# A hybrid decoder layer on one core: the scratch of rotated queries and keys laid out row by row, and TensorE and the SyncE queue issued in the order in which the program is written

## The chip, the core and the metric

The kernel runs on one core of a Trainium2 chip, in one launch. Its time is the device time in microseconds (us); several executions are timed, and one execution is recorded by the profiler. The engines are PE (TensorE; PEld is its loading of weights), DVE (VectorE), ACT (ScalarE), POOL (GpSimd) and SP (SyncE, which only issues transfers). ACT issues transfers too. Each engine works through its own list of instructions in order; 16 DMA engines carry out the transfers of all of them.

## The reference

One layer over 1024 positions of width 2048, in float32:

```python
h = rms_norm(x, norm_gain)
q, k, v, g_attn, xr, g_rec = jnp.split(h @ w_in, SPLITS, axis=-1)   # w_in: 2048 x 6144
q = rope(q.reshape(1, 1024, 8, 2, 64), cos, sin)                    # 8 heads, 2 maps of 64
k = rope(k.reshape(1, 1024, 8, 2, 64), cos, sin)
...                      # per head: w = softmax(q0 k0) - lam * softmax(q1 k1), causal
o = rms_norm(w @ v, subln_gain) * (1 - lam_init) * silu(g_attn)
r = rg_lru(causal_conv(xr, conv_w, conv_b), ...) * silu(g_rec)      # 8 blocks of 128
x = x + jnp.concatenate([o, r], -1) @ w_out                         # w_out: 2048 x 2048
return rms_norm(x, final_gain)
```

## The kernel before, in words

**Precision.** Every matmul operand is split into a rounded part (hi) and the rest (lo), and products are added as hi·hi, hi·lo and lo·hi, so a projection step of 128 inputs is three matmuls of 128x512 (`triple`, L364). `split` (L169) makes hi on ACT (L170) and lo on DVE or POOL (L171).

**Order of the work.** The sequence is handled in two halves of 512 positions (b = 0 and 1; the attention calls them l). In each half the units of `UNITS` come one after the other: a head (four projections: two for the rotated queries and keys, then values and gate) or a recurrent block (two projections). Afterwards `outputs` does the output projection (L829). A projection takes four tiles of weights of 256 KB; each tile serves 12 matmuls (four triples).

Around the projections stand small tasks that are Python generators: `Slots` counts ticks, one per triple, and every `yield n` puts the rest of a task n ticks later into the written order. The weight task `stream` (L256) issues loads up to 6 tiles ahead of the split (`WAHEAD`), and splits up to 4 tiles ahead of their use (`WRING`). All buffers of 128x512 come from one list of 89 slots.

**The path that the change touches.** `rope` (L460) takes the two projections of queries and keys of a head. Their 128 rows are four groups of 32: map 0 and map 1 of the queries, then map 0 and map 1 of the keys. It rotates them into two tiles and splits both: four tiles, hi of the first and second (t2, t4) and lo of the first and second (t1, t3). They go through a scratch in DRAM, `fs`, stored from ACT (L471), so that a map of a head comes back as one operand of 128 rows. Six ticks after the stores the head is ready; `loader` (L610) then calls `head_load` (L585), which issues on SP (all through `load`, L156) the two key tiles, one per map, and four query tiles: per map one of the hi rows and one of the lo rows, each with its 64 rows twice, read with a broadcast of 2. For l = 1 the keys and values of the first half are loaded again as well. `SCORE_LEAD` ticks later (24 or 28) `score` (L619) starts: per 128 positions, four or more matmuls into `sw` (L634 and L635; the second uses the lo queries), a masked maximum on DVE (L639), exponentials on ACT (L646), and on DVE the difference of the two softmaxes (L654). `weighted` (L679) then transposes the result in pairs of 128 positions (L758, into one bank, `tr`), splits it (L767, L768), and multiplies it with the values (L780 to L783). `head_out` (L718) normalises (L723, L726, L734, L737) and stores the rows `ms`.

**Who sets the order.** In the kernel before, a scheduler orders the instructions of each engine by its own model of time, with the written order as priority; so an engine's list can differ from the written one. The waits between engines and transfers are put in by the framework in either case.

Of the kernel before, what the change touches and what calls it, by code (L numbers as in the profile page):

```python
# [13 lines left out]
F32 = mybir.dt.float32  # L14
# [11 lines left out]
HALF = 512  # L26
# [81 lines left out]
class Trunk:  # L108
# [351 lines left out]
    def rope(self, b, h, ts):  # L460
        nc = self.nc
        t1, t2, t3, t4 = ts
        self.tt(t1.f, t1.f, t2.f, ALU.subtract)
        self.tt(t3.f, t3.f, t4.f, ALU.add)
        yield 1
        self.split(t1.f, t2, t1)
        self.split(t3.f, t4, t3)
        yield 4
        fs = self.dram.tile([4, 4, 32, HALF], F32, name=self.nm("fs"))
        for i, t in enumerate((t2, t4, t1, t3)):  # L470
            nc.scalar.dma_start(fs[:, i], t.f)  # L471
        self.rel(*ts)
        self.fs[h, b] = fs
        yield 6
        self.ready.add(("q", h, b))
# [109 lines left out]
    def head_load(self, h, l):  # L585
        k, q, v = [], [], []
        for c in range(l + 1):
            ks = []
            for m in range(2):
                kk = self.allocr()  # L590
                self.load(kk.f, self.fs[h, c][2 + m].rearrange("i r c -> (i r) c"))
                ks.append(kk)
            k.append(ks)
        for i in (0, 2):
            for m in range(2):
                t = self.allocr()
                src = self.fs[h, l][m, i:i + 2].rearrange("i r c -> (i r) c")
                self.load(t.f, src.unsqueeze(0).broadcast_to([2, 64, HALF]))
                q.append(t)
        if l:  # L600
            vs = []
            for d in self.vsc[h]:
                t = self.allocr()
                self.load(t.f, d)
                vs.append(t)
            v.append(vs)
        self.hd[h, l] = (k, q, v)
        self.loaded[h, l] = self.sl.now
# [261 lines left out]
            self.rel(y)  # L870

    def run(self):
        if True:
            self.consts()
            for gen in (self.stream(), self.loader(), self.scores(), self.weighted()):
                self.sl.spawn(gen)
            for b in range(2):
                for name in UNITS:
                    (self.head if name[0] == "h" else self.rec)(b, int(name[1]))
                self.final(b)  # L880
                self.outputs(b)
# [58 lines left out]
```

## Time and profile before

| | |
|---|---|
| time, median of 3 runs | 2099.34 us (2096.14 to 2101.21) |
| time of the profiled execution | 2100.45 us |
| its span, from the first to the last instruction | 2098.7 us |
| mean granted TensorE clock | 0.913 of full speed |
| busy: PE, PEld, DVE, ACT, POOL | 82%, 67%, 37%, 38%, 40% |
| moved by the DMA engines | 237.02 MB, 113 GB/s in the mean |
| loads from the scratch `fs` (SP) | 112 of 256 KB |
| stores to it (ACT) | 64 of 256 KB |

How to read it: PE is the busiest engine, but an average over stages; its idle time stands in stretches whose ends the profile puts down to a releaser, an engine or a transfer. The granted clock is that of TensorE alone, at one of two levels, 1.2 or 2.4 GHz (0.5 or 1.0 of full speed), so that a mean of 0.913 says that it was at the lower level for some 17% of the time.

### The profile page before, as it was taken

How to read it: one execution, taken by the hardware profiler on the slowest of the kernel's cores; microseconds unless marked ns; L12 is line 12 of the kernel's file. 1: busy time of each engine (PE TensorE's matmuls, PEld its weight loads, DVE VectorE, ACT ScalarE, POOL GpSimd, SP SyncE). 2: the span in 40 equal slices, each digit the busy share in tenths (PEclk: the TensorE clock that was granted, in tenths of full speed). 3: DMA queues.
4: the chain of work that ended last, by engine and by line, in shares of the span. 5: the costliest groups of instructions: out<-in, count | busy, mean ns of one | idle time of the engine just before them, and what ended most of it. 6: DMA issues, size and time to landing. Idle time of an engine off the chain costs nothing.

```text
span 2098.7 us, 22044 instructions
## 1 busy us (share of the span) xinstructions
PE 1724.3 (82%) x7716; PEld 1408.4 (67%) x7716; DVE 779.1 (37%) x1333; ACT 804.7 (38%) x1393; POOL 849.8 (40%) x710
## 2 busy tenths in 40 slices
PE   7758868787786779989979787878787879799996
PEld 5646756566665667768867576767676767587885
DVE  8515342414151325741115242424252515265101
ACT  6215242525161236633414342525252424365321
POOL 7313433434342325765632242424233333266560
PEclk9879989898898889999989898989898999899998
DMA  5432333333323235423652242323233232255312
GB/s 209 135 112 74 109 97 110 94 105 93 120 79 120 79 98 170 159 81 99 214 185 84 79 119 81 113 90 113 91 106 97 90 115 83 89 181 188 113 63 80
DMA packets 131502, 237.02 MB, mean 113 GB/s; under 512 B 13248, under 2 KB 17472, under 8 KB 131392
## 3 DMA queue, kind: packets, MB, share of 16 engines
q1 hardware_dynamic: 116032, 206.27, 31.6%
q10 hardware_dynamic: 15360, 29.36, 4.0%
q8 instruction: 60, 0.98, 0.2%
q14 instruction: 50, 0.41, 0.1%
HBM read 197.83 MB, written 37.75 MB: 112 GB/s over the span
## 4 chain that ended last, share of the span: by engine, by line
PE 31%; DMA 14%; DVE 7%; ACT 3%; issue 2%; SPq 2%; POOL 1%; ACTq 0%; POOLq 0%; DVEq 0%
PE pq L368 11%; PE pq L829 8%; PE sw L829 8%; DMA fs<-b 5%; DMA b<-fs 4%; DMA b<-w_in 4%; SPq L156 2%; DVE b L174 2%; DMA ms<-b 1%; PE pq L758 1%; DVE sw L639 1%; ACT wide L646 1%; DVE b L533 1%; ACT b L170 1%; DVE wide L654 1%
## 5 line engine op out<-in xcount | busy, mean ns | idle before, releaser
L368 PE MATMUL pq<-b,b 128*128 128x512 f32 x4512 | 1151.6, 408 | 83.7 <-DVE b L171 64.0
L171 POOL TENSOR_TENSOR b<-b,b 128x512 fp32r<-128x512 f32 x504 | 671.9, 1347 | 1033.0 <-ACT b L170 720.8
L368 PEld LDWEIGHTS pq<-b,b 128*128 128x128 f32 x4512 | 871.5, 198 | 263.9 <-DVE b L171 67.8
L170 ACT CAST b<-b 128x512 fp32r<-128x512 f32 x592 | 349.2, 617 | 962.2 <-DMA b<-w_in 390.5
L829 PE MATMUL pq<-b,b 128*128 128x512 f32 x768 | 197.6, 393 | 4.4 <-DVE wide L174 4.4
L829 PE MATMUL sw<-b,b 128*128 128x512 f32 x768 | 197.0, 392 | 0.0
L174 DVE TENSOR_TENSOR b<-pq,b 128x512 f32<-128x512 f32 x113 | 74.8, 686 | 276.6 <-PE pq L368 180.9
L829 PEld LDWEIGHTS pq<-b,b 128*128 128x128 f32 x768 | 144.8, 189 | 35.8 <-DVE wide L174 4.8
L829 PEld LDWEIGHTS sw<-b,b 128*128 128x128 f32 x768 | 145.6, 190 | 30.6
L174 POOL TENSOR_TENSOR b<-b,b 128x512 f32<-128x512 f32 (+1 forms) x98 | 126.4, 1291 | 65.2 <-DVE b L740 29.0
L635 PE MATMUL sw<-b,b 128*128 128x512 f32 (+2 forms) x192 | 70.7, 377 | 83.8 <-DMA b<-fs 83.8
L646 ACT ACTIVATE wide<-sw,mx 128x128 f32<-128x128 f32 (+7 forms) x128 | 93.9, 737 | 88.0 <-DVE mx L642 50.1
L639 DVE CUSTOM_DVE_ANT_0 sw<-sw,mask 128x128 f32<-128x128 f32 (+7 forms) x128 | 95.2, 774 | 79.6 <-PE sw L635 79.6
L758 PE MATMUL pq<-ident,wide 128*128 128x128 f32 x288 | 56.0, 304 | 66.9 <-DVE wide L654 63.2
L634 PE MATMUL sw<-b,b 128*128 128x512 f32 (+2 forms) x192 | 69.4, 367 | 40.5 <-DMA b<-fs 33.2
L635 PEld LDWEIGHTS sw<-b,b 128*128 128x128 f32 x192 | 38.4, 200 | 94.3 <-DMA b<-fs 88.9
L171 DVE TENSOR_TENSOR b<-b,b 128x512 fp32r<-128x512 f32 x88 | 88.9, 1033 | 29.3 <-ACT b L170 26.0
L455 DVE SCALAR_TENSOR_TENSOR b<-b,b 128x512 f32<-128x512 f32 x32 | 31.1, 971 | 178.0 <-ACT b L453 178.0
L758 PEld LDWEIGHTS pq<-ident,wide 128*128 128x128 f32 x288 | 38.0, 154 | 85.9 <-DVE wide L654 73.0
L768 DVE TENSOR_TENSOR b<-pq,b 128x512 fp32r<-128x512 f32 (+1 forms) x80 | 50.9, 636 | 103.6 <-ACT b L767 96.7
L767 ACT CAST b<-pq 128x512 fp32r<-128x512 f32 (+1 forms) x80 | 43.2, 540 | 99.3 <-PE pq L758 89.7
L634 PEld LDWEIGHTS sw<-b,b 128*128 128x128 f32 x192 | 38.2, 199 | 49.2 <-issue 30.3
(130 smaller groups left out, 1345.8 us busy)
## 6 DMA issues: line engine op xcount, KB each, us to landing
b<-w_in SPq DMA_DIRECT2D x384, 256.0 KB
b<-w_out SPq DMA_DIRECT2D x128, 256.0 KB
b<-fs SPq DMA_DIRECT2D x112, 256.0 KB
fs<-b ACTq DMA_DIRECT2D x64, 256.0 KB
b<-xt SPq DMA_DIRECT2D x32, 256.0 KB
ms<-b ACTq DMA_DIRECT2D x32, 256.0 KB
b<-ms SPq DMA_DIRECT2D x32, 256.0 KB
wide<-x SPq DMA_DIRECT2D x20, 256.0 KB
```

What stands on the lines that cost most here:

```text
L170: self.nc.scalar.copy(hi.r, x)
L171: (eng or self.nc.vector).tensor_tensor(out=lo.r, in0=x, in1=hi.f, op=ALU.subtract)
L174: (eng or self.nc.vector).tensor_tensor(out=out, in0=a, in1=b, op=op)
L368: self.nc.tensor.matmul(acc, lhsT=x.r[:, s], rhs=y.r, start=kt == 0 and j == 0, stop=kt == KT - 1 and j == 2)
L634: nc.tensor.matmul(o, lhsT=q[m].r[:, qs], rhs=kk, start=True, stop=False)
L635: nc.tensor.matmul(o, lhsT=q[2 + m].r[:, qs], rhs=kk, start=False, stop=True)
L639: nc.vector.tensor_tensor_reduce(out=s, in0=s, in1=self.mask[:, 896 - off:896 - off + cols], scale=1.0, scalar=NEG, op0=ALU.add, op1=ALU.m ...
L646: nc.scalar.activation(p[:, :cols], self.swide[m][:, :cols], AF.Exp, scale=QK ** -0.5, bias=mx[:, m:m + 1], accum_out=sm[:, m:m + 1])
L758: nc.tensor.transpose(self.tr[:, c:c + P], ws[qi][:, kb * P:(kb + 1) * P], self.ident)
L767: nc.scalar.copy(wh.r[:, first:], self.tr[:, first:])
L768: nc.vector.tensor_tensor(out=wl.r[:, first:], in0=self.tr[:, first:], in1=wh.f[:, first:], op=ALU.subtract)
L829: nc.tensor.matmul(accs[t], lhsT=x.r[:, s], rhs=z.r, start=i == 0 and j == 0, stop=i == KT - 1 and j == 2)
```

## The change

The scratch of a head is now indexed group, row, block, column: each of its 32 rows in a group holds six blocks of 512 side by side, the four tiles (hi, hi, lo, lo) and, for the two query groups, the two hi tiles once more. A store writes 128 rows of 2 KB at a distance of 12 KB; two more stores of 64 rows each (L473 of the changed kernel, 128 KB) write the second copies. A load takes four neighbouring blocks of 32 rows: keys blocks 0 to 3, queries blocks 0 to 3 and then 2 to 5. So an operand has its 128 rows in another order than before, the same for keys and queries, and the two matmuls of a score give hi·hi + lo·lo and lo·hi + hi·lo. There are as many loads, of the same size, and no broadcast. And PE and SP keep the written order instead of the scheduler's; DVE, ACT and POOL are still ordered by the scheduler.

```diff
--- before.py
+++ after.py
@@ -466,9 +466,11 @@
         self.split(t1.f, t2, t1)
         self.split(t3.f, t4, t3)
         yield 4
-        fs = self.dram.tile([4, 4, 32, HALF], F32, name=self.nm("fs"))
+        fs = self.dram.tile([4, 32, 6, HALF], F32, name=self.nm("fs"))
         for i, t in enumerate((t2, t4, t1, t3)):
-            nc.scalar.dma_start(fs[:, i], t.f)
+            nc.scalar.dma_start(fs[:, :, i].rearrange("g r c -> (g r) c"), t.f)
+        for i, t in enumerate((t2, t4)):
+            nc.scalar.dma_start(fs[:2, :, 4 + i].rearrange("g r c -> (g r) c"), t.f[:64])
         self.rel(*ts)
         self.fs[h, b] = fs
         yield 6
@@ -588,14 +590,13 @@
             ks = []
             for m in range(2):
                 kk = self.allocr()
-                self.load(kk.f, self.fs[h, c][2 + m].rearrange("i r c -> (i r) c"))
+                self.load(kk.f, self.fs[h, c][2 + m, :, :4])
                 ks.append(kk)
             k.append(ks)
         for i in (0, 2):
             for m in range(2):
                 t = self.allocr()
-                src = self.fs[h, l][m, i:i + 2].rearrange("i r c -> (i r) c")
-                self.load(t.f, src.unsqueeze(0).broadcast_to([2, 64, HALF]))
+                self.load(t.f, self.fs[h, l][m, :, i:i + 4])
                 q.append(t)
         if l:
             vs = []
@@ -870,7 +871,8 @@
             self.rel(y)
 
     def run(self):
-        if True:
+        engines = {mybir.EngineType.PE, mybir.EngineType.SP}
+        with self.tc.manual_schedule(engines=engines):
             self.consts()
             for gen in (self.stream(), self.loader(), self.scores(), self.weighted()):
                 self.sl.spawn(gen)
```

**PE, in the first half, the last pair of transposes of a head** (before: L758, changed: L759; `sw` are the scores, `wide` the softmax differences of positions 256 to 383 (wide_74) and 384 to 511 (wide_76), L368 the projections). Before:

```order
L635 MATMUL sw_71<-b_2328,b_2336 128x512
...
L368 MATMUL pq_69<-b_172,b_2634 128x512
L758 MATMUL pq_66<-ident,wide_74 128x128
L368 MATMUL pq_69<-b_288,b_2661 128x512
...
L368 MATMUL pq_69<-b_392,b_2685 128x512
L758 MATMUL pq_66<-ident,wide_76 128x128
L758 MATMUL pq_66<-ident,wide_74 128x128
L758 MATMUL pq_66<-ident,wide_76 128x128
```

and of the change:

```order
L636 MATMUL sw_71<-b_2338,b_2346 128x512
...
L368 MATMUL pq_69<-b_174,b_2644 128x512
L759 MATMUL pq_66<-ident,wide_74 128x128
L759 MATMUL pq_66<-ident,wide_76 128x128
L759 MATMUL pq_66<-ident,wide_74 128x128
L759 MATMUL pq_66<-ident,wide_76 128x128
L368 MATMUL pq_69<-b_290,b_2671 128x512
...
L368 MATMUL pq_69<-b_302,b_2672 128x512
L759 MATMUL pq_66<-ident,wide_76 128x128
L759 MATMUL pq_66<-ident,wide_74 128x128
L759 MATMUL pq_66<-ident,wide_76 128x128
```

Each "..." stands for further rows of L368 alike. What moved: of the four transposes of the first step, three stood behind 13 more projection matmuls, and now all four stand in one piece directly behind the 18 that follow the scores; the nine matmuls after them come before the three of the second step. The same holds in the second half, where it was 8 matmuls. Elsewhere PE's list reads almost as before.

**SP, in the first half, the loads of the third head** (fs_1637 is its scratch before, fs_1643 in the change). Before, with 69 loads of w_in ahead of the first of them:

```order
L156 DMA b_1985<-w_in 128x512
L156 DMA b_1800<-w_in 128x512
L156 DMA b_1874<-w_in 128x512
L156 DMA b_1675<-fs_1637 128x1x512
L156 DMA b_1677<-fs_1637 128x1x512
L156 DMA b_1671<-fs_1637 128x512
L156 DMA b_1673<-fs_1637 128x512
L156 DMA b_1679<-fs_1637 128x1x512
L156 DMA b_1681<-fs_1637 128x1x512
L156 DMA b_1852<-w_in 128x512
L156 DMA b_1908<-w_in 128x512
L156 DMA b_2079<-w_in 128x512
```

and of the change, with 60 loads of w_in ahead:

```order
L156 DMA b_1621<-w_in 128x512
L156 DMA b_1653<-w_in 128x512
L156 DMA b_1671<-w_in 128x512
L156 DMA b_1679<-fs_1643 128x1x512
L156 DMA b_1681<-fs_1643 128x1x512
L156 DMA b_1683<-fs_1643 128x1x512
L156 DMA b_1685<-fs_1643 128x1x512
L156 DMA b_1687<-fs_1643 128x1x512
L156 DMA b_1689<-fs_1643 128x1x512
L156 DMA b_1701<-w_in 128x512
L156 DMA b_1718<-w_in 128x512
```

What moved: the six loads of a head stand nine weight tiles earlier, in one piece, and the weight tiles come one after the other in the order of use. PE's first score of that head stands behind the matmuls of 57 tiles in both lists.

## Rows read from the trace of the kernel before

**Rows 1.** The head of the page and its line of busy times: per engine the busy time in us, its share of the span and the number of instructions.

```profile
span 2098.7 us, 22044 instructions
...
PE 1724.3 (82%) x7716; PEld 1408.4 (67%) x7716; DVE 779.1 (37%) x1333; ACT 804.7 (38%) x1393; POOL 849.8 (40%) x710
```

**Rows 2.** What TensorE waited for in the whole run: the waiting line and tile, what released it, then the sum in us, the number of times and the longest one in us.

```profile
PE sw L635 <- DMA b<-fs: 83.8, 17, 9.3
PE pq L368 <- DVE b L171: 64.0, 7, 12.3
PE pq L758 <- DVE wide L654: 63.2, 22, 5.4
PE pq L726 <- ACT b L723: 44.1, 3, 14.8
PE sw L634 <- DMA b<-fs: 33.2, 6, 8.8
...
PE pq L737 <- DVE hs L734: 8.7, 2, 7.8
```

**Rows 3.** TensorE in order of time in the first half of the sequence (b = 0), around the scores of one head: start in us, us, engine, line, operation and shape, count; in brackets the idle time before it in us and what ended it.

```profile
365.13 0.55 PE L634 MATMUL sw<-b,b 128*128 128x256 f32 x1 [4.18 <-DMA b<-fs]
372.81 0.58 PE L635 MATMUL sw<-b,b 128*128 128x256 f32 x1 [7.13 <-DMA b<-fs]
...
377.96 0.58 PE L635 MATMUL sw<-b,b 128*128 128x256 f32 x1 [4.36 <-DMA b<-fs]
378.34 8.58 PE L368 MATMUL pq<-b,b 128*128 128x512 f32 x30
...
411.82 0.27 PE L758 MATMUL pq<-ident,wide 128*128 128x128 f32 x1
411.85 3.21 PE L368 MATMUL pq<-b,b 128*128 128x512 f32 x13
418.13 0.55 PE L758 MATMUL pq<-ident,wide 128*128 128x128 f32 x3 [3.08 <-DVE wide L654]
```

**Rows 4.** The same stretch on the queue of ScalarE: the stores to the scratch of rotated queries and keys (columns as in rows 3).

```profile
338.60 0.53 ACTq L471 DMA_DIRECT2D fs<-b  x1
...
339.69 2.74 ACTq L471 DMA_DIRECT2D fs<-b  x3
```

**Rows 5.** The queue of SyncE in the second half (b = 1), between the stores of one head and its scores: start in us, time from the first to the last issue in us, line and transfer, count.

```profile
1482.11 1.17 SPq L156 DMA_DIRECT2D b<-fs  x2
1484.64 5.44 SPq L156 DMA_DIRECT2D b<-w_in  x1
1490.17 7.04 SPq L156 DMA_DIRECT2D b<-fs  x4
1497.25 10.15 SPq L156 DMA_DIRECT2D b<-w_in  x5
```

**Rows 6.** Busy time by stretch: the stretch, its length in us, busy us of PE, PEld, DVE, ACT and POOL with the number of instructions, then the granted TensorE clock, the busy share of the 16 DMA engines, and GB/s. In order: a stretch of loads at the start; the four stores of rows 4 under way; loads of queries alone under way; the wait of rows 3; the output projection and the first projections after it, without a wait.

```profile
5.00:10.00 5.00, 2.75 (x6) 1.66 (x6) 3.27 (x8) 3.21 (x7) 0.47 (x1) 1.00 0.98 343
345.00:350.00 5.00, 5.00 (x26) 4.15 (x25) 0.69 (x1) 0.62 (x1) 0.90 (x1) 1.00 0.26 100
360.00:365.00 5.00, 0.95 (x5) 0.45 (x3) 0.00 (x0) 0.00 (x0) 0.00 (x0) 0.97 0.13 51
360.90:378.30 17.40, 1.73 (x5) 1.13 (x5) 0.00 (x0) 0.00 (x0) 0.00 (x0) 0.61 0.38 128
...
950.00:1050.00 100.00, 100.00 (x442) 82.79 (x442) 15.71 (x33) 39.87 (x81) 62.12 (x50) 1.00 0.51 164
```

**Rows 7.** The chain of work that ended last, in order of time, in one period of the second half: start in us, us, what.

```profile
1472.84 0.53 ACTq L471
...
1474.22 10.36 DMA fs<-b
...
1490.17 0.47 SPq L156
1490.69 0.59 SPq L156
...
1491.99 20.01 DMA b<-fs
1512.05 0.80 PE sw L635
```

**Rows 8.** The same chain around 1325 to 1345 us: a store of 256 KB to the contiguous scratch of the mixed rows.

```profile
1329.29 4.88 DMA ms<-b
```

**Rows 9.** TensorE in the second half, columns as in rows 3: at the first scores of one head, at the transposes of its last pair, and at the weights ahead of the scores of the next head, which is that of rows 5 and 7.

```profile
1402.63 0.80 PE L635 MATMUL sw<-b,b 128*128 128x512 f32 x1 [2.35 <-DMA b<-fs]
...
1403.65 7.97 PE L368 MATMUL pq<-b,b 128*128 128x512 f32 x30
...
1440.39 0.27 PE L758 MATMUL pq<-ident,wide 128*128 128x128 f32 x1
1440.42 2.07 PE L368 MATMUL pq<-b,b 128*128 128x512 f32 x8
1447.90 0.90 PE L758 MATMUL pq<-ident,wide 128*128 128x128 f32 x3 [5.41 <-DVE wide L654]
...
1501.35 7.28 PE L368 MATMUL pq<-b,b 128*128 128x512 f32 x24 [10.17 <-DVE b L171]
1508.46 0.39 PE L634 MATMUL sw<-b,b 128*128 128x512 f32 x1
```

**Rows 10.** ScalarE in the second half, at the end of one head and at the stores of a later one (that of rows 7), columns as in rows 3.

```profile
1173.08 0.62 ACT L170 CAST b<-b 128x512 fp32r<-128x512 f32 x1 [18.85 <-DMA b<-w_in]
1173.60 0.58 ACT L722 COPY b<-pq 128x512 f32<-128x512 f32 x1
1174.08 0.60 ACT L723 ACTIVATE b<-pq 128x512 f32<-128x512 f32 x1
...
1472.84 3.08 ACTq L471 DMA_DIRECT2D fs<-b  x4
```

**Rows 11.** VectorE in the first half, after the last scores of the head of rows 3, columns as there.

```profile
408.29 1.21 DVE L563 SCALAR_TENSOR_TENSOR b<-b,b 128x512 f32<-128x512 f32 x1
409.42 1.77 DVE L455 SCALAR_TENSOR_TENSOR b<-b,b 128x512 f32<-128x512 f32 x1
411.12 0.68 DVE L639 CUSTOM_DVE_ANT_0 sw<-sw,mask 128x512 f32<-128x512 f32 x1
```


## The prediction

> **What bounds the kernel now.** I read the busy times first: PE is busy for 1724.3 of 2098.7 us, and no other engine for more than 40% [rows 1]. So the time is PE's work plus PE's waits, about 374 us, and the question is what ends them. The list of PE's waits sorts them [rows 2]. Scores wait for loads from the scratch: 83.8 + 33.2 = 117.0 us. Projections wait for the lo part of a weight tile: 64.0. Transposes wait for the softmax difference: 63.2. The head's normalisation waits on ACT and DVE: 44.1 + 8.7 = 52.8.
>
> The first group is seen at one head: before its scores PE stands for 4.18, 7.13 and 4.36 us [rows 3]. The stores were issued from 338.60 us on, yet the last query tile came only at 377.96 [rows 3, 4]. The reader is to see the rate meanwhile: with the stores under way the DMA engines are busy to 0.26 of 16, some four engines, at 100 GB/s; with query loads alone to 0.13, some two engines, at 51 GB/s; plain loads at the start use 0.98 and move 343 GB/s [rows 6]. So the transfers through the scratch are slow because few engines carry them, not because the engines are full.
>
> The second and fourth group come from the same place. In the second half SP issues two loads from the scratch, one weight tile, and four more; one weight issue lasts 5.44 us and the four take 7.04, so that the next weight tiles go out at 1497.25 [rows 5], and PE stands for 10.17 us before the projection at 1501.35 [rows 9]. At another head ACT stands 18.85 us at a cast that waits for a weight tile, with the two readings of the head's result (L722, L723) behind it [rows 10]; PE waits for L723 three times, up to 14.8 us [rows 2]. The chain of waits confirms it: in one period of the second half it runs from the first store at 1472.84 through 10.36 us of store, SP, and 20.01 us of load to the scores at 1512.05, 39.2 us [rows 7].
>
> **The change part by part, against the profiled 2100.45 us** (1.1 above the median of the runs; 0.2%, 4 us, is about what a measurement tells from no change).
>
> *Layout: the handoff from store to load.* New: six stores instead of four, six or eight loads of 256 KB as before. Issue: four stores took 3.08 us, 0.77 each [rows 10], so six take 4.6. The landing of the last: a 256 KB store to a contiguous scratch takes 4.88 [rows 8], against 10.36 here. Then six loads; a load that isn't held up is issued in about 0.5 to 0.6 us [rows 7], 3.5 in all, and I give its landing the 4.88 of the store, as the nearest row. Sum 17.9 us. From both sides: no shape like it is in the trace, so 1.57 MB of loads take between 4.6 us at 343 GB/s and 30.8 at 51 [rows 6]. I take the fast end, since the new accesses have 128 rows or 32 groups of rows in front, as the plain loads have 128, and no leading 2 or 4, which is what the two slow shapes share.
> The Trainium skill, "DMA: Bandwidth & Descriptors", has this as a rule (section "Why a DMA increments its semaphore by 16 and not by 1", and "Rules for kernel authors"): a transfer runs on the largest number of engines up to 16 that divides the slowest dimension of both sides, and a leading broadcast of c copies keeps it to c. By it the new transfers get 16 and the sum is the one above; with two engines it would be that of rivals 3 and 4. The trace agrees for the old shapes (two and four engines); no run yet shows the new ones.
>
> *What hides it.* PE comes to the first scores in the first half 22.3 us after the first store (338.60 to 360.9, where the wait begins) [rows 3, 4, 6]; in the second half (1508.46 − 10.17) − 1472.84 = 25.5 us, once the wait of 10.17 is gone [rows 7, 9]. 17.9 fits into both (two loads more in the second half make it 19), with 4 us to spare in the first. Longer than 22 us, and part of the wait is back. The written order helps here: the loads stand nine weight tiles earlier on SP. It has a price there: what is queued behind them are weight tiles, and only 60 instead of 69 are issued ahead. PE uses a tile in 12 × 0.226 = 2.7 us (442 matmuls in 100 us [rows 6]). When the first store goes out PE is 22.3 / 2.7, about 8 tiles, before the scores, at tile 49; SP is free again some 13 us later (4.6 + 4.88 + 3.5), at tile 54, and the 61st is needed six tiles on, 16 us. That cover holds against a cast of 0.62 [rows 10] and a transfer of 4.88. With the old handoff of 39.2 us it would not.
>
> The terms, taken as gone entirely: waits for the scratch 117.0, for weights 64.0, at the head's normalisation 52.8 [rows 2].
>
> *The clock.* After such a wait PE runs on at the lower of its levels (1.2 instead of 2.4 GHz): the granted clock is 0.61 in the stretch of the wait [rows 6], and the 30 matmuls behind it take 8.58 us instead of 30 × 0.226 = 6.8 [rows 3], 1.8 more. In the second half 24 take 7.28 instead of 5.4, 1.9 more, and 30 after the wait for the scratch 7.97, 1.2 more [rows 9]. Eight heads × 1.8, seven waits for weights × 1.9, five for the scratch × 1.2, and 1.9 for each of the three at L723: 14.4 + 13.3 + 6.0 + 5.7 = 39.4 us.
>
> *PE in the written order.* It differs only at the transposes. The four of a last pair now wait together for the softmax of its second block. Before, 13 matmuls (2.9 us) stood ahead of the waiting three and the wait was 3.08 [rows 3]; in the second half 8 matmuls (1.8 us) and 5.41 [rows 9]. Worst case, all of it is added: 8 × 2.9 + 8 × 1.8 = 37.6 us. Best case nothing: on VectorE two operations of 1.21 and 1.77 us stand between the two maxima of that softmax [rows 11], and the listing of DVE has both ahead of them in the change. Neither bound is nearer; I take half, 19 us.
>
> *Two more stores per head*, 32 issues of 0.77 us on ACT, cost nothing of their own: ACT is busy for 38% [rows 1], and they are in the 17.9 above. Bytes: 16 heads × 0.25 MB more written, 4.2 MB, 12 us of transfers at 343 GB/s, spread over the span with the engines mostly idle.
>
> *Start, output projections, end:* these take no part; 950 to 1050 us already runs without a wait at the full clock [rows 6].
>
> **Sum.** 117.0 + 64.0 + 52.8 + 39.4 − 19 = 254.2; 2100.45 − 254.2 = 1846 us.
>
> **The rivals.**
> 1. *The weights stay late.* The loads get fast, but SP in the written order reaches them early and stands until the stores land, with weights queued behind. For it: SP's list, 60 tiles instead of 69. Against: the 16 us of cover. Then the 64.0 and 52.8 stay with their share of the clock (13.3 + 5.7): 1846 + 135.8 = 1982 us.
> 2. *The softmax becomes the bound.* PE's strict order costs the full 37.6 us and each of the 16 waits brings one more slow stretch of 1.9: 1846 + 18.6 + 30.4 = 1895 us. For it: this is the largest wait that remains. Against: DVE's new list.
> 3. *Slower: PE's order without the gain of the layout.* At the last transposes of each head 13 or 8 ready projections are held behind a wait; price 37.6 + 30.4 = 68, so 2168 us. It decides only if the transfers give back less than 68 us, that is if the new loads still run on some two engines; rows 6 show that rate for a leading broadcast of 2, which the change no longer has, hence the small chance; the same holds for rival 4.
> 4. *No change.* The loads stay on few engines and the order of PE costs nothing, as its list is nearly the old one: 2100 us.
>
> **How the numbers follow.** Forecast 0.69; rival 1 0.11, rival 2 0.13, rival 3 0.04, rival 4 0.03. Faster 0.93, same 0.03, slower 0.04. Low end: the 63.2 us of softmax waits go as well and the 19 are not paid: 2100.45 − 273.2 − 63.2 = 1764; I write 1760. High end: half of the 116.8 us of weights and normalisation stays, 58, on top of rival 2: 1895 + 58 = 1953; I write 1955. The range leaves out rivals 1, 3 and 4, 0.18.
>
> **What would show it.** Right: in PE's list of waits no row for the scratch above some 10 us in sum, none above 10 for the lo parts and for L723; the store part of the chain near 5 us instead of 10.36; a mean granted clock above 0.95; the transposes' wait between 63 and 101 us and now the largest. Wrong: stretches with loads from the scratch alone at 51 GB/s again (rivals 3, 4); waits on SP for the stores with PE waiting for L171 or ACT for weights (rival 1); transposes above 100 us (rival 2).

## The result, and the profile after

The changed kernel takes **1845.7 us** (median of 4 runs, 1843.55 to 1849.77) against 2097.74 for the kernel before, run beside it: ratio 0.8805 (95% interval 0.8776 to 0.8833). The forecast was 1846. The profiled execution took 1846.63 us, its span is 1844.5, its mean granted clock 0.962 (before 0.913).

The head of the page, the busy times, and the shares of the chain that ended last:

```profile
span 1844.5 us, 22031 instructions
...
PE 1689.6 (92%) x7716; PEld 1386.2 (75%) x7716; DVE 784.8 (43%) x1333; ACT 826.8 (45%) x1404; POOL 863.5 (47%) x710
...
PE 44%; issue 6%; DVE 5%; ACT 4%; POOL 2%; DMA 1%; ACTq 0%; POOLq 0%; DVEq 0%
```

PE's idle time fell from 374.4 to 1844.5 − 1689.6 = 154.9 us, and its busy time by 34.7 with the same 7716 matmuls, which is the clock. What PE waited for (columns as in [rows 2]):

```profile
PE pq L759 <- DVE wide L655: 71.2, 29, 5.5
...
PE pq L738 <- DVE hs L735: 4.9, 3, 2.0
...
PE pq L368 <- DVE b L171: 1.4, 1, 1.4
```

The reader is to see what is missing against [rows 2]: no row for the scratch, L171 at 1.4 instead of 64.0, no row for the normalisation at L727 (L726 before), and the transposes at the top with more times (29 instead of 22).

One head of the first half in order of time (columns as in [rows 3]). The stores on ACT's queue, which answer to [rows 4]:

```profile
282.56 1.95 ACTq L471 DMA_DIRECT2D fs<-b  x4
284.55 1.44 ACTq L473 DMA_DIRECT2D fs<-b  x2
```

SP's queue, from the loads of this head on:

```profile
288.33 3.96 SPq L156 DMA_DIRECT2D b<-fs  x6
292.38 3.33 SPq L156 DMA_DIRECT2D b<-w_in  x5
```

PE, from this head's first scores to the transposes of its last pair, which answers to [rows 3]:

```profile
304.76 0.28 PE L635 MATMUL sw<-b,b 128*128 128x256 f32 x1
...
305.23 6.99 PE L368 MATMUL pq<-b,b 128*128 128x512 f32 x30
...
332.68 4.25 PE L368 MATMUL pq<-b,b 128*128 128x512 f32 x18
336.77 0.27 PE L759 MATMUL pq<-ident,wide 128*128 128x128 f32 x1
342.01 0.90 PE L759 MATMUL pq<-ident,wide 128*128 128x128 f32 x3 [4.96 <-DVE wide L655]
342.56 2.91 PE L368 MATMUL pq<-b,b 128*128 128x512 f32 x6
```

The loads are all issued by 292.3 us, 9.7 after the first store; the scores start at 304.76, 22.2 after it, without a wait, and the 30 matmuls behind them take 6.99 us instead of 8.58 [rows 3]. The transposes stand for 4.96 us with no projection between the first and the other three, and six matmuls afterwards take 2.91 us, 0.49 each, at the lower clock (the granted clock is 0.50 from 342.0 to 345.5 us).

The list of transfers (queue, count, KB each, median us from issue to landing):

```profile
b<-fs SPq DMA_DIRECT2D x112, 256.0 KB, 4.4
fs<-b ACTq DMA_DIRECT2D x64, 256.0 KB, 2.3
fs<-b ACTq DMA_DIRECT2D x32, 128.0 KB, 2.7
```

Busy time by stretch, columns as in [rows 6]: the stores of this head under way, its six loads being issued, and the last of them landing together with the five weight tiles that were issued from 292.38 us on:

```profile
282.56:288.30 5.74, 5.74 (x27) 4.76 (x26) 1.30 (x2) 0.57 (x1) 0.00 (x0) 1.00 0.70 231
288.33:292.30 3.97, 3.97 (x20) 3.27 (x19) 0.69 (x1) 0.00 (x0) 0.00 (x0) 1.00 0.61 173
292.50:297.00 4.50, 4.50 (x23) 3.74 (x22) 0.69 (x1) 0.59 (x1) 0.00 (x0) 1.00 0.87 279
```

Against [rows 6] the busy share is 0.70 instead of 0.26 with stores under way, and 0.61 instead of 0.13 with loads from the scratch nearly alone. A mean of 0.61 of 16 engines takes at least ten of them, one of 0.70 at least twelve.

### The profile page after: what moved, and what is told of

It reads as the page before. It is cut to its first block, busy times and chain, and to the rows that moved or that the text cites. A ratio compares the mean times of both kernels' runs of the same rounds, so it can differ in the third digit from the quotient of the medians.

```text
span 1844.5 us, 22031 instructions
## 1 busy us (share of the span) xinstructions
PE 1689.6 (92%) x7716; PEld 1386.2 (75%) x7716; DVE 784.8 (43%) x1333; ACT 826.8 (45%) x1404; POOL 863.5 (47%) x710
## 2 busy tenths in 40 slices
DMA packets 135726, 241.23 MB, mean 131 GB/s; under 512 B 15424, under 2 KB 19648, under 8 KB 135616
## 4 chain that ended last, share of the span: by engine, by line
PE 44%; issue 6%; DVE 5%; ACT 4%; POOL 2%; DMA 1%; ACTq 0%; POOLq 0%; DVEq 0%
PE pq L368 21%; PE pq L830 9%; PE sw L830 9%; ACT wide L647 1%; DVE sw L640 1%; POOL b L171 1%; PE pq L759 1%; POOL b L174 1%; ACT b L170 1%; DMA ms<-b 1%; DVE wide L655 1%; DVE b L565 1%; PE sw L636 1%; PE sw L635 1%; PE pq L738 1%
## 5 line engine op out<-in xcount | busy, mean ns | idle before, releaser
L368 PE MATMUL pq<-b,b 128*128 128x512 f32 x4512 | 1124.1, 402 | 19.1 <-DVE b L174 9.2
L171 POOL TENSOR_TENSOR b<-b,b 128x512 fp32r<-128x512 f32 x504 | 680.8, 1370 | 705.1 <-ACT b L170 363.4
L368 PEld LDWEIGHTS pq<-b,b 128*128 128x128 f32 x4512 | 857.5, 194 | 194.0 <-DVE b L174 9.6
L170 ACT CAST b<-b 128x512 fp32r<-128x512 f32 x592 | 352.7, 619 | 587.5 <-DMA b<-w_in 103.5
L830 PE MATMUL pq<-b,b 128*128 128x512 f32 x768 | 198.3, 394 | 4.4 <-DVE b L174 2.2
L830 PEld LDWEIGHTS pq<-b,b 128*128 128x128 f32 x768 | 145.5, 190 | 37.1 <-DVE b L174 3.1
L830 PEld LDWEIGHTS sw<-b,b 128*128 128x128 f32 x768 | 145.1, 189 | 30.4
L174 POOL TENSOR_TENSOR b<-b,b 128x512 f32<-128x512 f32 (+1 forms) x98 | 131.1, 1339 | 59.4 <-DVE b L741 24.3
L759 PE MATMUL pq<-ident,wide 128*128 128x128 f32 x288 | 57.0, 309 | 73.1 <-DVE wide L655 71.2
L759 PEld LDWEIGHTS pq<-ident,wide 128*128 128x128 f32 x288 | 38.6, 157 | 90.8 <-DVE wide L655 82.6
L171 DVE TENSOR_TENSOR b<-b,b 128x512 fp32r<-128x512 f32 x88 | 83.9, 976 | 39.1 <-ACT b L170 35.2
L174 DVE TENSOR_TENSOR wide<-pq,wide 128x512 f32<-128x512 f32 x12 | 8.2, 691 | 167.8 <-PE pq L830 127.1
L635 PE MATMUL sw<-b,b 128*128 128x512 f32 (+2 forms) x192 | 64.7, 345 | 0.0
L636 PE MATMUL sw<-b,b 128*128 128x512 f32 (+2 forms) x192 | 64.1, 345 | 0.0
L655 DVE SCALAR_TENSOR_TENSOR wide<-wide,mx,wide 128x128 f32<-128x128 f32 (+3 forms) x64 | 55.1, 862 | 2.0
L767 POOL MEMSET b<- 128x128 f32 x64 | 12.7, 204 | 91.2 <-PE pq L368 59.4
```

The costliest lines, as they stand in the source:

```text
L170: self.nc.scalar.copy(hi.r, x)
L171: (eng or self.nc.vector).tensor_tensor(out=lo.r, in0=x, in1=hi.f, op=ALU.subtract)
L174: (eng or self.nc.vector).tensor_tensor(out=out, in0=a, in1=b, op=op)
L368: self.nc.tensor.matmul(acc, lhsT=x.r[:, s], rhs=y.r, start=kt == 0 and j == 0, stop=kt == KT - 1 and j == 2)
L635: nc.tensor.matmul(o, lhsT=q[m].r[:, qs], rhs=kk, start=True, stop=False)
L636: nc.tensor.matmul(o, lhsT=q[2 + m].r[:, qs], rhs=kk, start=False, stop=True)
```

## The experiments

The theory to be tested was the prediction's: the layout gives the whole gain (273 us), the written order of PE takes a little of it back (19). The rival was that the order costs much more, or that SP's order is what makes the gain. Each median is of four runs (of five in e6); ratios are to the kernel before on the same chip, and 0.01 of a ratio is 21 us. The two rows in the middle keep the old scratch and take its slow stores or its slow loads apart by other edits than the change's, shown below.

| scratch | scheduled | SP written | PE written | both written |
|---|---|---|---|---|
| as before | 1 | 1.0506 (1.0486 to 1.0526) | 1.0184 (1.0165 to 1.0203) | 1.073 (1.0697 to 1.0763) |
| old, stores split (e13, e6) | 0.954 (0.9519 to 0.9561) | | | 1.0052 (1.0032 to 1.0072) |
| old, loads without the broadcast (e12, e5) | 0.8827 (0.881 to 0.8843) | | | 0.9328 (0.9307 to 0.9349) |
| as changed | 0.8541 (0.8522 to 0.8561) | 0.8496 (0.8468 to 0.8525) | 0.8846 (0.8823 to 0.887) | 0.8805 (the change) |

### The layout alone, and with one of the two engines written

e1_layout_only, against the changed kernel:

```diff
-        engines = {mybir.EngineType.PE, mybir.EngineType.SP}
-        with self.tc.manual_schedule(engines=engines):
+        if True:
```

> The changed kernel with the scheduler's order on PE and SP again, as before. Theory A (the layout is the gain; the order only costs at the transposes): 1846 - 19 = 1827 us, 1815 to 1845; no PE wait for the scratch, none for the lo parts of weights (L171) or L723 above 10 us in sum, the transposes' wait back from 71 to about 63 us. Rival B (the order carries part of the gain, since the scheduler's SP list has the loads of a head behind nine more weight tiles): 1900 to 1980 us, with PE waiting for the scratch at the first scores of each head again.

Measured: 1792.39 us, ratio 0.8541; span 1792.6, PE busy 1667.9, clock 0.972. That is below the range of Theory A, 1815 to 1845. The layout alone gives 306 us, not 273, and the order as a whole costs 53 us here (55 by the ratios), not 19. Of the 306, 374.4 − 124.7 = 249.7 are idle time of PE and 1724.3 − 1667.9 = 56.4 busy time, the clock.

e3_layout_sp and e4_layout_pe keep the layout and write the order of one engine, SP (shown) and PE:

```diff
-        engines = {mybir.EngineType.PE, mybir.EngineType.SP}
+        engines = {mybir.EngineType.SP}
```

> The changed kernel with only SP in the written order, PE by the scheduler. Theory A: PE's list costs what the transposes wait more, so as with the scheduler on both: 1827 us, 1815 to 1845, transposes' wait about 63 us. If SP's order is what matters (rival B), it equals the changed kernel or is better by PE's 19, 1825 to 1846, while the one without SP's order is at 1900 or more.

> The changed kernel with only PE in the written order, SP by the scheduler. Theory A: as the changed kernel, 1846 us, 1835 to 1860, transposes' wait about 71 us. Rival B: 1900 or more, with PE waiting for the scratch or for weights.

Measured: 1783.16 us (0.8496) with SP written, 1857.67 us (0.8846) with PE written; the first is again below its range, the second within. So the cost is PE's: by the ratios 65 us between e3 and the change, 64 between e1 and e4. SP's written order gives 9 us in either pair, at the edge of what the intervals tell apart. PE of e3 in order of time, at the transposes that were shown above of the change:

```profile
327.59 4.25 PE L368 MATMUL pq<-b,b 128*128 128x512 f32 x18
331.67 0.28 PE L759 MATMUL pq<-ident,wide 128*128 128x128 f32 x1
331.70 3.21 PE L368 MATMUL pq<-b,b 128*128 128x512 f32 x13
338.00 0.55 PE L759 MATMUL pq<-ident,wide 128*128 128x128 f32 x3 [3.08 <-DVE wide L655]
338.30 2.05 PE L368 MATMUL pq<-b,b 128*128 128x512 f32 x5
```

The scheduler lets 13 matmuls pass and PE waits 3.08 us, as before the change [rows 3]; the five behind the wait take 0.41 each.

### The order alone

e2_order_only, e8_order_sp and e9_order_pe are the kernel before with both engines (shown), SP alone or PE alone written:

```diff
-        if True:
+        engines = {mybir.EngineType.PE, mybir.EngineType.SP}
+        with self.tc.manual_schedule(engines=engines):
```

> The kernel before (old layout, loads with the leading broadcast) with PE and SP in the written order. Theory A: the handoff is as slow as before, 39 us of which PE hides 22, and the order costs 19 to 68 us at the transposes: 2120 us, 2100 to 2170; query loads at 51 GB/s. Rival B: the loads stand nine tiles earlier on SP, so part of the waits goes: 1980 to 2060 us.

Measured: 2249.75 us, ratio 1.073, 151 us slower; PE idle 488.8 us, clock 0.891. Neither the 19 nor the 68 us that the prediction put on the order can be that, so the two engines were taken apart:

> The kernel before with only SP in the written order. Theory A (with slow transfers, the written SP order is what loses: weight tiles stand behind the loads with 60 instead of 69 issued): 2250 less the 54 us that PE's order cost with the new layout = 2196 us, 2170 to 2230, with ACT waiting for weights and PE for ACT. Rival B (SP's order gains as with the new layout, and PE's order is what loses): 2080 to 2110.

Measured: 2201.94 us, ratio 1.0506. Rows of what PE waited for in this run:

```profile
PE sw L635 <- DMA b<-fs: 181.2, 24, 11.4
PE sw L634 <- ACT wide L646: 63.3, 13, 18.5
...
PE pq L780 <- ACT b L767: 47.5, 2, 24.1
...
PE sw L634 <- DMA b<-fs: 14.7, 9, 3.6
```

The first row of SP's waits:

```profile
SPq L156 <- DMA fs<-b: 556.9, 32, 41.4
```

And of ACT's:

```profile
ACT b L170 <- DMA b<-w_in: 516.9, 28, 40.8
```

SP reaches the loads early and stands for the stores 556.9 us in sum (187.8 before), with the weights queued behind; ACT's casts then wait 516.9 us for weights (390.5 before), and what stands behind them on ACT, the exponentials and the splits of the transposes, keeps PE waiting (63.3 and 47.5 us). This is the mechanism of the prediction's rival 1, on the old layout; but PE pays for it in other rows than rival 1 named (L171 and L723 are not in the list any more), and its waits for the scratch itself grew most, from 117.0 to 181.2 + 14.7 = 195.9 us. No run takes these two apart.

> The old layout with PE alone in the written order; SP is scheduled. Theory: PE's written order costs what it cost under the new layout (between the run with SP alone written and the change, 63 us; between the layout alone and PE written, 65), because the transposes of a last pair are held behind the softmax whatever the scratch does, less what the scratch's own waits hide of it: 2098 + 54 = 2150 us, range 2115 to 2175, with PE's wait of the transposes for the softmax near 80 us instead of 63. Rival A: the scratch's waits swallow it, since PE would stand for the next head's loads anyway: 2098 within 10. Rival B: the run with both engines written (2250) is PE's order and not SP's, although SP alone written came to 2202: then 2200 or more. With the run of SP alone (2202) the two orders add up if this one is near 2098 + 48 = 2146.

Measured: 2134.59 us, ratio 1.0184, 39 us slower. In the list of PE's waits the transposes' row for the softmax is 83.3 us (63.2 before):

```profile
PE pq L758 <- DVE wide L654: 83.3, 29, 5.5
```

It is less than the 64 us that the same order costs on the new layout, and in the lower half of the range, as it would be if rival A held for a part. The two orders add up: 0.0506 + 0.0184 = 0.069, against 0.073 together.

### The loads' and the stores' shape, with both engines written

Both kernels keep the old scratch `[4, 4, 32, HALF]` and its key loads. e5_loads_only keeps the old stores and takes the broadcast from the query loads, so that a head has ten loads, eight of them of half the size:

```diff
                 src = self.fs[h, l][m, i:i + 2].rearrange("i r c -> (i r) c")
-                self.load(t.f, src.unsqueeze(0).broadcast_to([2, 64, HALF]))
+                self.load(t.f[:64], src)
+                self.load(t.f[64:], src)
```

> Old scratch and its stores (leading 4), both engines in the written order, but each query tile loaded by two transfers of 64 rows instead of one with a leading broadcast of 2: the loads are fast, the stores as slow as before. Theory A (the loads on two engines are the larger part): handoff 3.1 + 10.4 for the stores and 5.5 + 4.9 for ten loads = 24 us against the 22 to 25 that PE hides: 1870 us, 1845 to 1900, beside 2250 for the old transfers in this order. Rival B (stores on four engines cost as much as the loads): 2000 to 2100.

Measured: 1955.56 us, ratio 0.9328; that is outside, and 110 us above the change. The loads are quick (10 are issued in 5.83 us), but SP only comes to them 14 us after the first store, 309.20 on ACT's queue and 323.26 on SP's. In order of time, ACT's queue:

```profile
309.20 2.97 ACTq L471 DMA_DIRECT2D fs<-b  x4
```

and SP's, which issues nothing in the 14 us:

```profile
323.26 5.83 SPq L156 DMA_DIRECT2D b<-fs  x10
```

Busy time by stretch in between (columns as in [rows 6]):

```profile
310.00:315.00 5.00, 5.00 (x23) 4.14 (x23) 0.50 (x1) 0.00 (x0) 0.00 (x0) 1.00 0.25 62
315.00:320.00 5.00, 5.00 (x25) 4.16 (x25) 0.69 (x1) 0.01 (x1) 0.00 (x0) 1.00 0.26 103
```

The old stores keep the DMA engines busy to 0.25 and 0.26, as in [rows 6]. SP's waits for the stores come to 567.0 us in this run, 417.2 in the change. PE hardly waits for the scratch itself (6.5 us): the price is paid through the exponentials, 46.5 us at the scores, behind ACT's late casts.

e6_stores_only keeps the broadcast loads and takes the stores apart, 16 of 32 rows for a head:

```diff
-            nc.scalar.dma_start(fs[:, i], t.f)
+            for g in range(4):
+                nc.scalar.dma_start(fs[g, i], t.f[32 * g:32 * g + 32])
```

> Old scratch, both engines in the written order, each of the four stores of a head split into four of 32 rows, so that no store has a leading 4; the query loads keep the leading broadcast of 2. Theory A: handoff 8 for 16 issues + 4 for the landing + 20 for the loads = 32 us, 10 us more than PE hides; the order-only kernel is 17 us short per head and 404 us above the changed kernel, so 10 us short is some 240 us: 2090 us, 2040 to 2160, query loads alone at 51 GB/s. Rival B: 1900 to 1980.

Measured: 2104.42 us, ratio 1.0052, as expected. The loads of one head from the scratch on SP's queue:

```profile
344.21 13.02 SPq L156 DMA_DIRECT2D b<-fs  x6
```

Busy time in a stretch while these loads run:

```profile
355.00:360.00 5.00, 2.33 (x11) 1.69 (x9) 0.92 (x2) 0.63 (x1) 0.00 (x0) 1.00 0.13 51
```

What PE waited for in the whole run, first row:

```profile
PE sw L636 <- DMA b<-fs: 131.6, 24, 9.1
```

The broadcast alone brings the 0.13 and 51 GB/s of [rows 6] back, and holds SP 13.02 us for six issues (3.96 in the change).

### The same two shapes under the scheduler

e12_loads_only_sched and e13_stores_only_sched are the last two with all engines scheduled: e12 has the loads of e5, e13 the stores of e6.

> The old stores, and each query load as two loads of 64 rows, both engines scheduled. Theory: the slow stores cost 110 us under the written order because SP stands for them with the weight tiles behind; with SP scheduled, 69 instead of 60 tiles are issued ahead of the loads, and the cost is smaller: 1792 + 38 = 1830 us, 1800 to 1870, and SP's waits for the stores well under the 567 us of the written one. Rival: the stores are slow by themselves and PE waits for them whatever SP's order is: 1900 us or more, with a wait of the scores for the scratch above 50 us.

> Each store as four stores of 32 rows, the old broadcast query loads, both engines scheduled. Theory: the broadcast loads run on some two engines and hold the scores and SP's queue, so most of what the layout gives stays lost: 2030 us, 2000 to 2060, with a wait of the scores for the scratch of 60 us or more. Rival: with quick stores the loads start early enough to be hidden, and the loss in the written order (2104 us) was PE's and SP's order: below 1950 us.

Measured: 1850.1 us (0.8827) and 1999.28 us (0.954, a hair under its range). SP waits 211.7 us for the stores in e12 (567.0 in e5), and PE of e13 waits 92.0 us in the scores' row for the scratch. So under the scheduler the loads' shape is worth 1 − 0.8827 or 246 us, the stores' shape 97 us alone and 0.8827 − 0.8541 or 60 us on top of the loads; with both engines written it is worth 110 us on top. (Both figures on top are against the new layout, which has six loads where e5 and e12 have ten, so they hold that difference too.) Written order costs 151 us on the old layout, 105 to 107 with one of the two shapes mended, 53 to 55 with both.

### Later turns

e10_later_turn is the change with the last pair's turn four ticks later (and the head's output four ticks instead of two); e11_later_turn_sp the same with only SP written.

```diff
+                    if pr == 1:
+                        yield 4
...
-        yield 2
+        yield 4
```

> The changed kernel with the written order itself moved at two places towards the scheduler's: four ticks (12 matmuls) more ahead of the transposes of a head's last pair, and four instead of two ticks between the square root of the normalisation and the matmuls of L738. Theory A (PE's order costs 54 us because ready projections stand behind the transposes and L738): the transposes' wait falls from 71 to some 40 us, that at L738 from 4.9 to 1, the granted clock rises from 0.962 to 0.97: 1795 us, 1780 to 1812. Rival B (the cost lies elsewhere, or later transposes hold back the scores behind them): 1830 or more.

> The change with the last pair's turn moved four ticks later and the head's output four ticks instead of two, and SP alone in the written order. Theory: the moved turns paid 34 us because they gave a strictly ordered PE ready projections ahead of the transposes; a scheduled PE has them ahead anyway, so 1783 as the run with SP alone written, 1770 to 1795. Rival: the turns help by giving VectorE and ScalarE more time before the transposes, whoever orders PE; then 20 to 34 us faster, 1750 to 1763.

Measured: 1811.71 us (0.8642, 0.8629 to 0.8655), 34 us under the change and at the upper edge of its range; and 1771.2 us (0.8452, 0.8433 to 0.8471), 9 us under e3 and 74 under the change, the quickest kernel of the study. PE of e10 in order of time, at the transposes of the first half:

```profile
325.42 6.97 PE L368 MATMUL pq<-b,b 128*128 128x512 f32 x30
...
336.96 0.90 PE L761 MATMUL pq<-ident,wide 128*128 128x128 f32 x3 [4.47 <-DVE wide L655]
```

Here the time was not won as expected: 30 matmuls now stand ahead instead of 18, 2.7 us more, yet the wait is 4.47 instead of 4.96, since the softmax is ready later too (336.96 is 11.4 us after the last score, in the change it was 9.2). Of the 36.7 us between the two spans, 21.2 are idle time (154.9 and 133.7 us) and 15.5 busy time (1689.6 and 1674.1), and three places have most of them. From the first scores of the last head but one to the end it takes 352.3 us instead of 362.8; there three waits of the change of 2.72, 1.88 and 2.50 us become 0.73, nothing and 0.43. From the last head of the first half to the first of the second it takes 323.5 instead of 331.1, and from the second head's first scores to the third's 81.2 instead of 87.4. In sum the wait for the softmax falls from 71.2 to 59.4 us, where some 40 were expected, and the clock rises from 0.962 to 0.972. In e11 the moved turns still bring 9 us, so not all that they do is for a strict order. Which of the two moved turns does it was not taken apart.

## Why the prediction was right, and where only its sum was

**The cause and the handoff: right.** Of the waits that were to go (117.0 + 64.0 + 52.8 = 233.8 us), 1.3 us are left in e1 and 6.3 in the change. The six loads are issued in 3.96 us and land after 4.4, so that the last of them lands some 14 us after the first store; the forecast was 17.9, with 22.3 to hide it, and 22.2 are there. The new loads came near the fast end of the bounds, at some 8.4 us between 4.6 and 30.8. The Trainium skill, "DMA: Bandwidth & Descriptors" (section "Why a DMA increments its semaphore by 16 and not by 1"), has a transfer run on the largest number of engines up to 16 that divides the slowest dimension of both sides. The trace agrees: 0.13 of 16 again in e6 for a leading 2, 0.25 in e5 for a leading 4, and 0.61 and 0.70 for the new loads and stores, more than eight engines could give.

**The layout's term: 273 forecast, 306 measured (e1).** The waits were priced well (249.7 us of idle time against 233.8; 5.6 of the difference are the transposes' wait, 57.6 instead of 63.2). The clock was not: 39.4 forecast, 56.4 measured. Where it lies is seen from the lines of PE with most of it (busy time in us, mean ns of one, then idle time before). Before:

```profile
L368 PE MATMUL pq<-b,b 128*128 128x512 f32 x4512 | 1151.6, 408 | 83.7 <-DVE b L171 64.0
...
L635 PE MATMUL sw<-b,b 128*128 128x512 f32 (+2 forms) x192 | 70.7, 377 | 83.8 <-DMA b<-fs 83.8
...
L634 PE MATMUL sw<-b,b 128*128 128x512 f32 (+2 forms) x192 | 69.4, 367 | 40.5 <-DMA b<-fs 33.2
```

and e1:

```profile
L368 PE MATMUL pq<-b,b 128*128 128x512 f32 x4512 | 1113.7, 398 | 18.6 <-DVE b L174 9.7
...
L635 PE MATMUL sw<-b,b 128*128 128x512 f32 (+2 forms) x192 | 65.2, 347 | 0.0
L636 PE MATMUL sw<-b,b 128*128 128x512 f32 (+2 forms) x192 | 64.2, 346 | 0.0
```

The sum priced projections behind a wait, and those gave back 37.9 us, near its 39.4. What it left out are the other matmuls that ran at the lower clock: the scores themselves gave back another 10.7 us, and the rest lies in smaller groups.

**PE's written order: 19 forecast, 64 to 65 measured (53 to 55 with SP's).** This is the term that failed. Part of its mechanism held: the transposes' wait grew to 71.2 us, from 57.6 in e1 and 50.4 in e3, in 29 instead of 21 or 22 pieces, and it is the largest, in the forecast's 63 to 101. Three things did not: half of the worst case was too little, the clock behind the waits had no place in the term, and PE's list does not differ "only at the transposes". Of the 61.4 us between the spans of e3 and the change 36.8 are idle time and 24.6 slower matmuls; the transposes' wait has 20.8 of the idle time, and waits that e3 lacks or has for under 1 us come up at L738 (4.9), L784 (3.1) and L548 (2.9).

Half of the worst case was taken on the ground that VectorE's list had two operations moved ahead of the maxima [rows 11]. They did move, as VectorE shows in order of time in the head that was shown above:

```profile
332.01 0.69 DVE L455 SCALAR_TENSOR_TENSOR b<-b,b 128x512 f32<-128x512 f32 x1 [0.70 <-ACT b L453]
332.62 0.69 DVE L565 SCALAR_TENSOR_TENSOR b<-b,b 128x512 f32<-128x512 f32 x1
333.22 0.69 DVE L640 CUSTOM_DVE_ANT_0 sw<-sw,mask 128x512 f32<-128x512 f32 x1
...
334.65 1.08 DVE L643 TENSOR_SCALAR mx<-mx 128x2 f32<-128x2 f32 x1
...
336.36 2.19 DVE L572 TENSOR_TENSOR_SCAN b<-b,carry,b 128x512 f32<-128x512 f32 x1
...
341.20 0.75 DVE L655 SCALAR_TENSOR_TENSOR wide<-wide,mx,wide 128x512 f32<-128x512 f32 x1
```

but the exponentials came hardly sooner, as ACT was then the late one; its rows in the same stretch:

```profile
333.54 1.28 ACT L568 ACT_TABLE_LOAD   x1
334.84 0.63 ACT L568 ACTIVATE b<-b 128x512 f32<-128x512 f32 x1
335.49 1.28 ACT L647 ACT_TABLE_LOAD   x1
336.78 0.69 ACT L647 ACTIVATE wide<-sw,mx 128x512 f32<-128x512 f32 x1
```

The maxima are done at 335.73 (L643), yet ACT loads a table for a recurrent block's L568 and then the exponentials' own, and starts at 336.78; on VectorE the scan of 2.19 us follows. Counted from the last score, the maxima are done after 2.9 us (4.5 in e3), the exponentials start after 3.9 (4.5 in e3). The difference was ready 9.1 us after the last score (332.85 to 341.95), in e3 10.2 (327.75 to 337.94). So 1.1 us came back for 2.9 lost, 1.8 a head. The six matmuls at 0.49 instead of 0.226 us are 1.6 too long, but e3's five at 0.41 had been 0.9 too long already, so the clock adds 0.7. That is 2.5 for this head, and its stretch to the next head's first scores is longer by that much (304.76 to 389.74 against 299.52 to 381.99). Ten such stretches (100.2 to 560.2 us and 1109.3 to 1481.7 in the change, 101.5 to 546.3 and 1076.2 to 1436.7 in e3) take 27 us more, 2.7 each in the mean.

In the second half the cost is hardly the wait that was priced. There the transposes of a last pair wait 3.0 to 3.1 us, against 3.4 to 4.2 in e3 and 4.9 to 6.4 in e1; yet four stretches take 11.9 us more than in e3, 6.3 of them busy time (347.92 and 341.62 us), the rest waits of which the transposes' have 1.

Another 27 of the 61 us between the two spans fall behind these stretches, up to the output projection (560.2 to 712.1 and 1481.7 to 1651.1 against 546.3 to 687.7 and 1436.7 to 1589.6), which the sum had not priced apart; fewer projections are left to pass there, but why these ends weigh as much was not tested.

**So the total came out by luck, from two errors that cancel:** 33 us too little for the layout, some 35 too little for the order. PE's order alone came nearly to the price of rival 2, to which the prediction gave 0.13 (68 us, 37.6 of waits and 30.4 of clock; measured 36.8 and 24.6), though by other waits than it named for much of it; with the layout's term as forecast that would have given 1895.

**SP's written order: nothing forecast, 9 us gained (at the edge of the intervals), and on slow transfers 106 lost.** The cover of the weights held in the change (ACT's wait for w_in 103.5 us, 390.5 before), although SP stands 417.2 us for the stores. e8 shows rival 1's mechanism, and e5 that it is there when only the stores are slow (SP stands 567.0 us for them, 211.7 in e12): the forecast's "with the old handoff it would not" was right, and the order pays only with the layout.

**Two more stores, more bytes: nothing, as forecast.** 241.23 instead of 237.02 MB moved; no wait in the lists names them. No run took them away.

**Signs.** The clock, the L171 and L723 rows and the rows for the scratch came as stated. The store part of the chain can't be compared, as the chain no longer passes through this scratch (DMA 1% of it); the landing of 2.3 us stands for it, under the 4.88 that was taken from [rows 8].

## What to carry to other kernels

Price a strict order by what stood behind each wait when the order was free: count each matmul that used to pass the waiting one as lost, as long as no row shows that what is waited for comes sooner (here 1.1 of 2.9 us came back at one head), add the slow clock behind the wait, and price the ends of a stage apart, which cost as much here as the middle. A queue kept in written order is only as good as the transfer that it waits for: here the same order of SP was worth 9 us with quick stores and loads and cost 106 with slow ones, so mend the transfer's shape first, then try one engine at a time. And a total that hits can hide two terms that miss, which the part alone (e1) shows in one run.

## What the runs showed of the hardware

- A slow load holds its queue at the issue as well: six loads, four of them with the broadcast, took SP 13.02 us to issue in e6, six loads of the same size without one 3.96 in the change.
- The stores of 128 KB took 2.7 us from issue to landing in the change, those of 256 KB 2.3, the loads of 256 KB from the scratch 4.4. The small stores are issued last, behind four others, so this does not show what half the bytes cost by themselves.
- A table load on ACT takes 1.28 us. In the head shown two of them stand between the maxima's operations and the exponentials, as a recurrent block's function comes in between, and the second ends 1.04 us after the maxima. No run took them away, so what the earlier maxima would be worth without them is open.
